# Layer 1's mixer: half of v and half of u as seven block products on normalized tiles

## The chip, the core and the metric

The kernel runs on one core of a Trainium2 chip. Its engines work side by side, each through its own list in order: TensorE (PE) multiplies, VectorE (DVE) and ScalarE (ACT) do elementwise work, GpSimd (POOL) some elementwise work and the issue of accumulating transfers, SyncE (SP) the issue of loads. They wait for each other by semaphores. The metric is the device time of one execution in microseconds (us).

## The reference

A trunk of two layers over 512 tokens of width 1024, in float32. Layer 0's mixer is a gated convolution beside a pooling, layer 1's a gMLP with spatial gating; each layer ends in a gated convolutional FFN of width 2816. What matters here is layer 1's mixer:

```python
def rms_norm(x, g):
    y = x * lax.rsqrt(jnp.mean(x * x, axis=-1, keepdims=True) + EPS)
    return y * g

def chunked_spatial_gating(u, v, sgu_norm, w_spatial, b_spatial):
    vn = rms_norm(v, sgu_norm).reshape(b, n, CHUNK, C_HEADS, C_HEAD_DIM)
    ws = w_spatial * mask                       # lower triangle
    gate = jnp.einsum('hts,bnshc->bnthc', ws, vn) + b_spatial.T[None, None, :, :, None]
    return u * gate.reshape(b, s, C_WIDTH)

xn = rms_norm(h, norm_mix[1])
proj = gelu(xn @ w_in_odd)                      # 1024 -> 2048
u, v = proj[..., :1024], proj[..., 1024:]
h = h + chunked_spatial_gating(u, v, ...) @ w_out_odd
```

## The kernel before

**Tiles.** The residual h lies as eight tiles `h[k]` of 128 features by 512 tokens. Each float32 operand of a matmul is split into two parts of the matmul's own type: `hi` is a copy by ACT, `lo` the remainder by DVE (`parts`, L131; `summed`, L122, gets the remainder by ACT and an accumulating transfer that POOL issues). A product of two such operands is three matmuls (`mm3`, L138): hi x hi, hi x lo, lo x hi. `hg[k]` holds the parts of `h[k]` times the norm's gain.

**The norm.** While the layer before ends, `Norm.add` (L179) makes the parts of `hg[k]` on ACT and DVE as soon as h[k] is added (L288), squares h[k] on ACT (L191) and adds the squares on POOL (L192, `ssq`). The factor r = 1/rms per token exists in two forms: as columns (`rstd_cols`, L205: four small matmuls over `ssq` into a bank called `ssc`, then a root) and spread over all partitions (`rstd_spread`, L195: four transposes into a bank called `ssr`, then a copy).

**Layer 1's mixer** (`mixer1`) computes v and u with tokens as output rows. Each is done in two halves of 512 columns, in the order v0, v1, u0, u1 (`in_group`, then `group`, L143): for each of eight feature tiles k and four token blocks j, `mm3` with 128x128 of `hg[k]` and a 128x512 piece of the weights, summed in four banks. That is 4 x 8 x 3 = 96 matmuls of 128x512 for each half. `hg` is not normalized, so r enters at the end as the scale of the Gelu on ACT; r's columns are made when the first bank of v0 is done. The spatial weights are loaded first, masked on POOL and turned by eight transposes inside v0 (`turn_spatial`). After v1 the columns of v's own norm give `vn`; after u0 come the eight spatial products (`spatial`, 3 matmuls each) and the first gatings (`gated`), and inside u1 the first four results are turned (`turned`) for the output projection `oo`.

**Layer FFNs.** They already use a form with seven block products for most of their width (`Ffn.both`): `Ffn.multiply` runs 4 x 3 matmuls of 128x256 for a product, and `Ffn.normalize` (L573) prepares normalized tiles, their parts and four block sums.

**What sets the order.** Loads go through SP's queue into four buffers (`raw`); a load is issued when the buffer's last reader is done. Weight parts have six buffers each. The program is recorded in the order of the code, and a scheduler then orders the instructions of each engine by its own costs, save those marked `inorder`; `behind` adds a constraint of order. The built order is fixed: on the chip each engine takes its list from the front. There are seven banks for products and one for small matters.

## Time and profile before

| | |
|---|---|
| timed runs, median | 997.9 us (997.45 to 998.35, three runs) |
| the profiled execution | 996.07 us |
| its span, first to last instruction | 994.4 us |
| mean granted TensorE clock | 0.998 |
| busy: PE, DVE, ACT, POOL | 99%, 70%, 53%, 10% |
| v0's first matmul | at 493.5 us |
| u0's first matmul | at 538.9 us |
| the last gelu of u1 starts | at 590.0 us |

The page of the profile is of one execution. Rows of a timeline give the start and the length in us, the engine, the line of the kernel, the operation, output<-inputs, the shape and a count; in brackets stands how long the engine had been idle before and what released it. A PE row's length holds the pipeline's depth, so the pace of matmuls is read from start to start.

### The profile page before, as it was taken

To read this page: it belongs to the slowest core of one execution; us is meant where nothing else is said; L and a number is where in the kernel's file an instruction comes from. 1 tells how busy PE (TensorE), PEld (TensorE's weight loads), DVE (VectorE), ACT (ScalarE), POOL (GpSimd) and SP (SyncE) were. 2 spreads that over 40 slices of the span, in tenths; PEclk is the share of its full clock that TensorE was granted. 3 is DMA by queue.
4 is the path that set the end of the run, shared out by engine and by line. 5 is a ranking of instruction groups with operands and counts; after the bars stand their busy time and mean duration, and the time that the engine had idled before them with its cause. 6 is when DMAs were issued, how large, how long until landed. Compare 5 with 4: busy or idle time off the path is not lost.

```text
span 994.4 us, 14683 instructions
## 1 busy us (share of the span) xinstructions
PE 983.6 (99%) x5811; PEld 872.0 (88%) x5811; DVE 699.4 (70%) x1053; ACT 523.9 (53%) x779; POOL 102.3 (10%) x120
## 2 busy tenths in 40 slices
PE   9999999999999999999999999999999999999997
PEld 6788888898989989899888888888989899898995
DVE  6887458967785877858943645399668768688676
ACT  5523346744653746537655344675546366363664
POOL 2131031200000000000300001211000010000100
PEclk9999999999999999999999999999999999999999
DMA  7342235554554645446333223435445456354542
GB/s 246 130 149 84 85 93 130 117 149 117 135 144 108 177 115 134 139 105 186 130 127 106 66 88 101 103 91 132 141 102 140 141 116 181 98 141 144 120 114 85
DMA packets 81904, 124.53 MB, mean 125 GB/s; under 512 B 4292, under 2 KB 53676, under 8 KB 81836
## 3 DMA queue, kind: packets, MB, share of 16 engines
q1 hardware_dynamic: 73004, 97.91, 30.8%
q0 software_dynamic: 6912, 23.07, 13.0%
q10 hardware_dynamic: 1920, 2.63, 0.8%
q8 instruction: 45, 0.74, 0.3%
q14 instruction: 23, 0.19, 0.1%
HBM read 98.42 MB, written 2.10 MB: 101 GB/s over the span
## 4 chain that ended last, share of the span: by engine, by line
PE 95%; DVE 2%; DMA 1%; issue 1%; ACT 0%; POOL 0%; SPq 0%; POOLq 0%; ACTq 0%
PE dn L139 4%; PE d L140 4%; PE d L139 4%; PE dn L140 4%; PE dn L141 4%; PE d L141 4%; PE gu L139 3%; PE gu L141 3%; PE gu L140 3%; PE v L139 1%; PE v L141 1%; PE u L139 1%; PE u L141 1%; PE oo L139 1%; PE oo L140 1%; PE oo L141 1%
## 5 line engine op out<-in xcount | busy, mean ns | idle before, releaser
L139 PE MATMUL dn<-whi_dn,a_hi 128*128 128x512 f32 x176 | 68.6, 390 | 0.0
L140 PE MATMUL d<-a_lo,whi_d 128*128 128x512 f32 x176 | 68.6, 390 | 0.0
L140 PE MATMUL dn<-wlo_dn,a_hi 128*128 128x512 f32 x176 | 68.6, 390 | 0.0
L141 PE MATMUL d<-a_hi,wlo_d 128*128 128x512 f32 x176 | 68.5, 389 | 0.0
L141 PE MATMUL dn<-whi_dn,a_lo 128*128 128x512 f32 x176 | 67.2, 389 | 0.0
L139 PE MATMUL d<-a_hi,whi_d 128*128 128x512 f32 x176 | 66.9, 390 | 0.0
L513 DVE SCALAR_TENSOR_TENSOR c<-rows,prm,c 128x512 f32<-128x512 f32 x88 | 65.4, 767 | 0.0
L127 POOL DMA_DIRECT2D wlo_g<-raw_g x22 | 19.1, 868 | 376.8 <-ACT wlo_g L126 362.6
L934 DVE TENSOR_TENSOR y<-dn,y 128x512 f32<-128x512 f32 x48 | 32.4, 685 | 23.3 <-PE dn L141 22.9
L126 ACT ACTIVATE wlo_g<-raw_g 128x1024 fp32r<-128x1024 f32 x22 | 23.2, 1055 | 42.3 <-PE dn L140 42.3
L135 DVE TENSOR_TENSOR wlo_u<-raw_u,whi_u 128x1024 fp32r<-128x1024 f32 x16 | 19.5, 1222 | 34.1 <-ACT whi_u L134 34.0
L519 ACT ACTIVATE s<-c,prm 128x512 f32<-128x512 f32 x44 | 30.9, 717 | 20.5 <-DVE c L513 20.4
L640 DVE TENSOR_TENSOR wlo_s34u<-s34u,whi_s34u 128x1024 fp32r<-128x1024 f32 x18 | 22.1, 1225 | 26.1 <-ACT whi_s34u L639 26.1
L639 ACT ACTIVATE whi_s12u<-s12u 128x1024 fp32r<-128x1024 f32 x18 | 18.9, 1051 | 39.5 <-PE d L140 33.7
L141 PEld LDWEIGHTS dn<-whi_dn,a_lo 128*128 128x128 f32 x176 | 33.0, 188 | 7.5 <-DVE a_lo L245 0.2
L140 PEld LDWEIGHTS d<-a_lo,whi_d 128*128 128x128 f32 x176 | 33.1, 188 | 7.2 <-DVE a_lo L245 0.2
L139 PEld LDWEIGHTS dn<-whi_dn,a_hi 128*128 128x128 f32 x176 | 33.1, 188 | 7.1 <-ACT a_hi L243 0.2
L288 DVE TENSOR_TENSOR h<-d,h 128x512 f32<-128x512 f32 x48 | 32.6, 684 | 9.3 <-PE d L141 9.3
L139 PEld LDWEIGHTS d<-a_hi,whi_d 128*128 128x128 f32 x176 | 32.9, 188 | 7.0
L141 PEld LDWEIGHTS d<-a_hi,wlo_d 128*128 128x128 f32 x176 | 33.0, 188 | 6.7
L140 PEld LDWEIGHTS dn<-wlo_dn,a_hi 128*128 128x128 f32 x176 | 33.1, 188 | 6.5
L192 POOL TENSOR_TENSOR ssq_f<-ssq_f,sq_f 128x512 f32<-128x512 f32 x14 | 18.9, 1348 | 180.8 <-ACT sq_f L191 145.9
(1195 smaller groups left out, 3414.8 us busy)
## 6 DMA issues: line engine op xcount, KB each, us to landing
raw_g<-in_w_ffn_gate_dram SPq DMA_DIRECT2D x36, 512.0 KB
raw_u<-in_w_ffn_up_dram SPq DMA_DIRECT2D x36, 512.0 KB
wlo_g<-raw_g POOLq DMA_DIRECT2D x22, 512.0 KB, 4.9
raw_d<-in_w_ffn_down_dram SPq DMA_DIRECT2D x22, 512.0 KB
raw_dn<-in_w_ffn_down_dram SPq DMA_DIRECT2D x22, 512.0 KB
wlo_u<-raw_u POOLq DMA_DIRECT2D x18, 512.0 KB, 5.0
raw_oe<-in_w_out_even_dram SPq DMA_DIRECT2D x8, 512.0 KB
raw_g<-in_w_ffn_gate_dram SPq DMA_DIRECT2D x16, 256.0 KB
```

Of the source, the lines that this page charges most:

```text
L126: nc.scalar.activation(lo, raw, AF.Copy, scale=-1.0)
L127: nc.gpsimd.dma_start(lo, raw, accum_op=ALU.add)
L135: behind(nc.vector.tensor_tensor(lo, raw, hi.bitcast(F32), ALU.subtract), after[0])
L139: nc.tensor.matmul(ps, lhs[0], rhs[0], start=start, stop=False)
L140: nc.tensor.matmul(ps, lhs[0], rhs[1], start=False, stop=False)
L141: nc.tensor.matmul(ps, lhs[1], rhs[0], start=False, stop=stop)
L192: nc.gpsimd.tensor_tensor(self.ssq, self.ssq, sq, ALU.add)
L288: nc.vector.tensor_tensor(h[k], ps, h[k], ALU.add)
L513: nc.vector.scalar_tensor_tensor(c, t[:, i : S + i], prm("cf", i * NF + ft), c, op0=ALU.mult, op1=ALU.add)
L519: nc.scalar.activation(s, c, AF.Silu, bias=self.prm("bf", ft))
L640: nc.vector.tensor_tensor(lo, src, hi.bitcast(F32), ALU.subtract)
L934: nc.vector.tensor_tensor(dst, ps, dst, ALU.add)
```

## The change

The first half of v (v0) stays a plain group, its feature tiles taken in the order 0, 4, 1, 5, 2, 6, 3, 7. r's columns are now made after 18 of its matmuls, and r is spread after 33. While v0 runs, `normalize(kp)` writes each pair of tiles again, normalized, in place in `hg[kp]` and `hg[kp + 4]`, and four sums and differences of their token halves (256 tokens each), with their parts, into `sums`; the first two pairs take `lo` by ACT and an accumulating transfer.

The second half of v (v1) and the first half of u (u0) are each computed by seven block products over blocks of 256 tokens, 512 features and 256 columns (`InProducts`), each of them in two halves of 128 tokens: 14 products of 4 x 3 matmuls of 128x256, with tokens as the stationary operand. The weights' sums are built in place in the raw buffers on DVE (L866 to L872 of the changed kernel). Seven weight parts take the place of four. Products 1, 6, 7 and 4 of a token half share a bank, which ACT copies out in between; DVE adds the others. Gelu comes without r's scale.

The second half of u (u1) stays a plain group on normalized tiles. The load of the spatial weights, their mask and their transposes move behind u0; all spatial products, the gatings of the first half and its transposes now stand between matmuls of u1 (`along`). `Ffn.multiply` becomes a wrapper of a free function `multiply` with the same instructions.

```diff
+    BANK = {1: "a", 6: "a", 7: "a", 4: "a", 5: "e", 3: "e", 2: "b"}
+    def multiply(banks, name, product, left, right):
+        at = BANK[product]
+        first = at not in banks
+        if first:
+            banks[at] = mm_bank(f"{name}{at}")
+        ps = banks[at][:, :HALF]
+        for kp in range(NP):
+            (a_hi, a_lo), (b_hi, b_lo) = left(kp), right(kp)
+            for l, r, end in ((a_hi, b_hi, False), (a_hi, b_lo, False),
+                              (a_lo, b_hi, kp == NP - 1)):
+                nc.tensor.matmul(ps, l, r, start=first, stop=end, skip_group_check=True)
+                first = False
+        return ps
...
+            chunks = {}
+            for kp in range(NP):
+                raw = wp.tile([P, 2, 512], F32, tag="raw", bufs=4, name=f"raw_v0_{kp}")
+                nc.sync.dma_start(raw, w[:, 1024:1536].rearrange(
+                    "(h k p) c -> p h k c", h=2, p=P)[:, :, kp])
+                hi, lo = parts(raw, 2, 512, f"v0_{kp}")
+                chunks[kp], chunks[kp + NP] = (hi[:, 0], lo[:, 0]), (hi[:, 1], lo[:, 1])
+            banks = {}
+            r = None
+            head = NK - 2
+            for i, j in ([(i, j) for i in range(head) for j in range(NT)]
+                         + [(i, j) for j in range(NT) for i in range(head, NK)]):
+                if (i, j) == (1, 2):
+                    norm.rstd_cols(inorder)
+                elif (i, j) == (2, 2):
+                    r = norm.rstd_spread(inorder)
+                k, cs = PAIRS[i], slice(j * P, (j + 1) * P)
+                if j not in banks:
+                    banks[j] = mm_bank(f"v0_{j}")
+                mm3(banks[j], (hg[k][0][:, cs], hg[k][1][:, cs]), chunks[k], i == 0, i == NK - 1)
+            work2 = [mp.tile([P, 2, S], F32, tag="v", bufs=4, name=f"nx{i}") for i in range(4)]
+            both = mp.tile([P, 4, S], F32, tag="u", bufs=2, name="nx4")
+            work2 += [both[:, :2], both[:, 2:]] * 2
...
+            sums = [[mp.tile([P, 2, 4, HALF], F32R, name=f"s{q}_{n}", **where)
+                     for n, where in enumerate(at)]
+                    for q, at in enumerate(((dict(tag="vn", bufs=4),) * 2,
+                                            (dict(tag="u", bufs=2), dict(tag="ws", bufs=1))))]
+            def halves(dst, src):
+                nc.scalar.activation(dst[0], src, AF.Copy)
+                nc.vector.tensor_tensor(dst[1], src, dst[0].bitcast(F32), ALU.subtract)
+            def normalize(kp):
+                x, t = work2[2 * kp], work2[2 * kp + 1]
+                for i, k in enumerate((kp, kp + NP)):
+                    nc.vector.scalar_tensor_tensor(x[:, i, :], h[k], prm1("mix", k), r,
+                                                   op0=ALU.mult, op1=ALU.mult)
+                halves(hg[kp], x[:, 0, :])
+                halves(hg[kp + NP], x[:, 1, :])
+                t = t.rearrange("p a (b c) -> p (a b) c", b=2)
+                a11, a21 = x[:, 0, :HALF], x[:, 0, HALF:]
+                a12, a22 = x[:, 1, :HALF], x[:, 1, HALF:]
+                nc.vector.tensor_tensor(t[:, 0, :], a21, a22, ALU.add)
+                nc.vector.tensor_tensor(t[:, 1, :], t[:, 0, :], a11, ALU.subtract)
+                nc.vector.tensor_tensor(t[:, 2, :], a11, a21, ALU.subtract)
+                nc.vector.tensor_tensor(t[:, 3, :], a12, t[:, 1, :], ALU.subtract)
+                hi, lo = (x[:, kp % 2] for x in sums[kp // 2])
+                if kp >= 2:
+                    halves((hi, lo), t)
+                    return
+                nc.scalar.activation(lo, t, AF.Copy, scale=-1.0)
+                nc.gpsimd.dma_start(lo, t, accum_op=ALU.add)
+                nc.scalar.activation(hi, t, AF.Copy)
+            SUM = {5: 0, 6: 1, 7: 2, 3: 3}
+            def tokens(product, i):
+                def at(kp):
+                    if product in SUM:
+                        cs = slice(i * P, (i + 1) * P)
+                        return tuple(x[:, kp % 2, SUM[product], cs] for x in sums[kp // 2])
+                    k = kp if product == 1 else kp + NP
+                    cs = slice((i + 2 * (product == 4)) * P, (i + 2 * (product == 4) + 1) * P)
+                    return hg[k][0][:, cs], hg[k][1][:, cs]
+                return at
+            class InProducts:
+                def __init__(self, name, c0, first=None):
+                    self.name, self.stat, self.first = name, {}, first
+                    self.raw = {}
+                    for i, j in ((0, 0), (1, 0), (0, 1), (1, 1)):
+                        self.raw[i, j] = fetch(
+                            w[i * 512 : (i + 1) * 512, c0 + j * HALF : c0 + (j + 1) * HALF]
+                            .rearrange("(k p) c -> p k c", p=P), 4, HALF, f"{name}_{i}{j}")
+                def plain(self):
+                    self.put(1, parts, (0, 0))
+                    self.put(2, summed, (1, 0))
+                def put(self, product, how, at):
+                    raw, a, b, name = self.raw[at]
+                    self.stat[product] = how(raw, a, b, f"{name}_{product}")
+                def rest(self):
+                    b11, b21, b12, b22 = (self.raw[at][0] for at in
+                                          ((0, 0), (1, 0), (0, 1), (1, 1)))
+                    behind(nc.vector.tensor_tensor(b12, b12, b11, ALU.subtract), self.first)
+                    self.put(5, parts, (0, 1))
+                    nc.vector.tensor_tensor(b12, b22, b12, ALU.subtract)
+                    self.put(6, parts, (0, 1))
+                    nc.vector.tensor_tensor(b11, b12, b11, ALU.subtract)
+                    self.put(7, parts, (0, 0))
+                    nc.vector.tensor_tensor(b21, b21, b12, ALU.subtract)
+                    self.put(4, parts, (1, 0))
+                    self.put(3, parts, (1, 1))
+                def run(self, out_, done):
+                    banks = ({}, {})
+                    e = {}
+                    for i, product in ((0, 1), (1, 1), (0, 2), (1, 2), (0, 6), (1, 6), (0, 5),
+                                       (0, 7), (1, 5), (1, 7), (0, 4), (0, 3), (1, 4), (1, 3)):
+                        hi, lo = self.stat[product]
+                        ps = multiply(banks[i], f"{self.name}_{i}", product, tokens(product, i),
+                                      lambda kp: (hi[:, kp, :], lo[:, kp, :]))
+                        c = {1: (0, 0), 2: (0, 0), 6: (0, 1), 3: (0, 1), 7: (1, 1), 5: (1, 1),
+                             4: (1, 0)}[product]
+                        dst = out_(i + 2 * c[0])[:, c[1] * HALF : (c[1] + 1) * HALF]
+                        if product in (1, 6):
+                            nc.scalar.copy(dst, ps)
+                        elif product == 5:
+                            e[i] = ps
+                        elif product == 7:
+                            nc.scalar.copy(dst, ps)
+                            self.last = nc.vector.tensor_tensor(dst, e[i], dst, ALU.add)
+                            nc.scalar.activation(dst, dst, AF.Gelu)
+                        elif product == 4:
+                            nc.scalar.activation(dst, ps, AF.Gelu)
+                            done(i + 2)
+                        else:
+                            nc.vector.tensor_tensor(dst, ps, dst, ALU.add)
+                        if product == 3:
+                            row = out_(i)
+                            nc.scalar.activation(row, row, AF.Gelu)
+                            done(i)
+            v1 = InProducts("v1", 1536)
+            v1.plain()
+            for kp in range(NP):
+                normalize(kp)
+            for t in range(NT):
+                nc.scalar.activation(v[t][:, :512], banks[t], AF.Gelu,
+                                     scale=norm.cols[:, t : t + 1])
+                v_square(0, t)
+            v1.rest()
...
+            v1.run(lambda t: v[t][:, 512:], lambda t: v_square(1, t))
+            u0 = InProducts("u0", 0, v1.last)
+            u0.plain()
...
             nc.vector.tensor_tensor(ssv[:, 0, :], ssv[:, 0, :], ssv[:, 1, :], ALU.add)
             rv = inv_sqrt_cols(ssv[:, 0, :], NT, "v")
...
+            v_normed(0)
...
-            in_group("u0", w, 0, False, u_done(0), 4)
-            for j in range(NK):
-                spatial(j)
-                if j < 4:
-                    gated(j)
-            def first_half(k):
-                if 2 <= k < 6:
-                    turned(k - 2)
-            in_group("u1", w, 512, False, u_done(1), 4, before=first_half)
+            u[0] = mp.tile([P, NT, S], F32, tag="u", bufs=2, name="u0")
+            u0.rest()
+            u0.run(lambda t: u[0][:, t, :], lambda t: None)
+            v_normed(1)
+            ws = wp.tile([P, NK, P], F32, tag="raw", bufs=4, name="ws")
+            nc.scalar.dma_start(ws, w_spatial[0].rearrange("h t s -> t h s"))
+            nc.gpsimd.affine_select(out=ws, in_=ws, pattern=[[0, NK], [-1, P]],
+                                    compare_op=ALU.is_ge, fill=0.0, base=0, channel_multiplier=1)
+            wsT = mp.tile([P, 2, NK, P], F32R, tag="ws", bufs=1, name="wsT")
+            wsT_hi, wsT_lo = wsT[:, 0], wsT[:, 1]
+            def turn_spatial(q):
+                ps = aux_bank(f"wst{q}")
+                for i in range(4):
+                    inorder(nc.tensor.transpose(ps[:, i * P : (i + 1) * P], ws[:, 4 * q + i, :],
+                                                ident))
+                hi = wsT_hi[:, 4 * q : 4 * q + 4, :]
+                pv = ps.rearrange("p (h t) -> p h t", t=P)
+                nc.scalar.activation(hi, pv, AF.Copy)
+                nc.vector.tensor_tensor(wsT_lo[:, 4 * q : 4 * q + 4, :], pv, hi.bitcast(F32),
+                                        ALU.subtract)
+            def along(k):
+                if k in (1, 2):
+                    turn_spatial(k - 1)
+                elif k == 4:
+                    for j in range(4):
+                        spatial(j)
+                        gated(j)
+                elif k in (6, 7):
+                    for j in (0, 1) if k == 6 else (2, 3):
+                        turned(j)
+                        spatial(j + 4)
+            def u1_done(t, ps):
+                nc.scalar.activation(u[1][:, t, :], ps, AF.Gelu)
+            u[1] = mp.tile([P, NT, S], F32, tag="u", bufs=2, name="u1")
+            in_group("u1", w, 512, False, u1_done, 4, before=along)
```

More of the change, by code (lines that the diff above doesn't have):

```diff
@@ L613, in moving @@
             return tuple(t[:, {4: 0, 5: 1}[product], :] for t in self.t41[kp])
-        BANK = {1: "a", 6: "a", 7: "a", 4: "a", 5: "e", 3: "e", 2: "b"}
         def multiply(self, banks, name, product, weights_):
-            at = self.BANK[product]
-            first = at not in banks
-            if first:
-                banks[at] = mm_bank(f"{name}{at}")
-            ps = banks[at][:, :HALF]
-            hi, lo = weights_
-            for kp in range(NP):
-                b_hi, b_lo = self.moving(product, kp)
-                a_hi, a_lo = hi[:, kp, :], lo[:, kp, :]
-                for l, r, end in ((a_hi, b_hi, False), (a_hi, b_lo, False),
-                                  (a_lo, b_hi, kp == NP - 1)):
-                    nc.tensor.matmul(ps, l, r, start=first, stop=end, skip_group_check=True)
-                    first = False
-            return ps
+            hi, lo = weights_
+            return multiply(banks, name, product, lambda kp: (hi[:, kp, :], lo[:, kp, :]),
+                            lambda kp: self.moving(product, kp))
         def unit(self, name):
@@ L761, in mixer1 @@
                                 .to_broadcast([P, 1, D]))
-            ws = mp.tile([P, NK, P], F32, tag="v", bufs=4, name="ws")
-            nc.scalar.dma_start(ws, w_spatial[0].rearrange("h t s -> t h s"))
-            nc.gpsimd.affine_select(out=ws, in_=ws, pattern=[[0, NK], [-1, P]],
-                                    compare_op=ALU.is_ge, fill=0.0, base=0, channel_multiplier=1)
-            wsT_hi = mp.tile([P, NK, P], F32R, name="wsT_hi")
-            wsT_lo = mp.tile([P, NK, P], F32R, name="wsT_lo")
@@ L768, in turn_spatial @@
-            def turn_spatial(k):
-                if k not in (3, 4):
-                    return
-                q = k - 3
-                ps = aux_bank(f"wst{q}")
-                for i in range(4):
-                    inorder(nc.tensor.transpose(ps[:, i * P : (i + 1) * P], ws[:, 4 * q + i, :],
-                                                ident))
-                hi = wsT_hi[:, 4 * q : 4 * q + 4, :]
-                pv = ps.rearrange("p (h t) -> p h t", t=P)
-                nc.scalar.activation(hi, pv, AF.Copy)
-                nc.vector.tensor_tensor(wsT_lo[:, 4 * q : 4 * q + 4, :], pv, hi.bitcast(F32),
-                                        ALU.subtract)
@@ L782, in mixer1 @@
-            rcol = []
-            def r_of(t):
-                if not rcol:
-                    rcol.append(norm.rstd_cols())
-                return rcol[0][:, t : t + 1]
+            chunks = {}
[5 more added lines that the diff above has]
+                chunks[kp], chunks[kp + NP] = (hi[:, 0], lo[:, 0]), (hi[:, 1], lo[:, 1])
@@ L789, in mixer1 @@
+            work2 = [mp.tile([P, 2, S], F32, tag="v", bufs=4, name=f"nx{i}") for i in range(4)]
+            both = mp.tile([P, 4, S], F32, tag="u", bufs=2, name="nx4")
+            work2 += [both[:, :2], both[:, 2:]] * 2
             v = [mp.tile([P, D], F32, tag="v", bufs=4, name=f"v{t}") for t in range(NT)]
             ssv = mp.tile([P, 4, PAD], F32, name="ssv")[:, :, :NT]
-            def v_done(half):
-                def done(t, ps):
-                    dst = v[t][:, half * 512 : (half + 1) * 512]
-                    nc.scalar.activation(dst, ps, AF.Gelu, scale=r_of(t))
-                    sq = tp.tile([P, S], F32, tag="sq", name=f"sqv{half}_{t}")
-                    nc.scalar.activation(sq, dst, AF.Square, accum_out=ssv[:, half, t : t + 1])
-                return done
@@ L800, in mixer1, with v_square @@
-            in_group("v0", w, 1024, False, v_done(0), 2, before=turn_spatial)
-            in_group("v1", w, 1536, False, v_done(1), 4)
+            def v_square(half, t):
+                sq = tp.tile([P, S], F32, tag="sq", name=f"sqv{half}_{t}")
+                nc.scalar.activation(sq, v[t][:, half * 512 : (half + 1) * 512], AF.Square,
+                                     accum_out=ssv[:, half, t : t + 1])
+            sums = [[mp.tile([P, 2, 4, HALF], F32R, name=f"s{q}_{n}", **where)
+                     for n, where in enumerate(at)]
+                    for q, at in enumerate(((dict(tag="vn", bufs=4),) * 2,
+                                            (dict(tag="u", bufs=2), dict(tag="ws", bufs=1))))]
@@ L805, in mixer1, with v_normed @@
             vn = []
-            for half in range(2):
+            def v_normed(half):
                 hi = mp.tile([P, NT, S], F32R, tag="vn", bufs=4, name=f"vnh{half}")
@@ L815, in mixer1 @@
                 vn.append((hi, lo))
+            v_normed(0)
             u, gt, mix = {}, {}, {}
-            def u_done(half):
-                u[half] = mp.tile([P, NT, S], F32, tag="u", bufs=2, name=f"u{half}")
-                def done(t, ps):
-                    nc.scalar.activation(u[half][:, t, :], ps, AF.Gelu, scale=r_of(t))
-                return done
             def by_chunk(ap):
```

## Prediction

> **What bounds the kernel now.** I read the page first: the busy shares and the chain that ended last.

> ```profile
> PE 983.6 (99%) x5811; PEld 872.0 (88%) x5811; DVE 699.4 (70%) x1053; ACT 523.9 (53%) x779; POOL 102.3 (10%) x120
> ...
> PE 95%; DVE 2%; DMA 1%; issue 1%; ACT 0%; POOL 0%; SPq 0%; POOLq 0%; ACTq 0%
> ```

> TensorE is busy for 99% of the span and carries 95% of the chain. Averages hide stages, so I read next the windows over layer 1's mixer (columns: window, length, then busy time and instruction count of PE, PEld, DVE, ACT, POOL, then the granted clock).

> ```profile
> 493.50:515.30 21.80, 21.80 (x105) 18.17 (x104) 12.55 (x16) 10.90 (x14) 4.62 (x4) 1.00 0.47 152
> 515.30:538.90 23.60, 23.60 (x105) 19.55 (x105) 3.71 (x4) 13.63 (x26) 0.00 (x0) 1.00 0.25 82
> 538.90:564.00 25.10, 25.10 (x112) 20.78 (x112) 14.45 (x23) 16.82 (x23) 0.00 (x0) 1.00 0.30 94
> 564.00:590.00 26.00, 26.00 (x124) 21.54 (x123) 11.64 (x17) 7.40 (x11) 0.00 (x0) 1.00 0.22 72
> ```

> In both halves of v and u PE is busy for the whole window, at full clock. Nothing there is waiting that the change could take away; it can gain only by shortening PE's own list, and it loses each wait it brings in. VectorE (DVE) has 3.7 of 23.6 us busy in the second half of v, which is the cover the change spends.

> **What PE saves.** The timeline of PE gives the pace of a 128x512 matmul, the chain that of a 128x256 one.

> ```profile
> 493.49 0.39 PE L139 MATMUL v<-whi_v,hgh 128*128 128x512 f32 x1
> ...
> 497.57 0.39 PE L139 MATMUL v<-whi_v,hgh 128*128 128x512 f32 x1
> ```
> ```profile
> 203.31 1.44 PE u_4a L630 x12
> ```

> From 493.49 to 497.57 stand 18 matmuls: 4.08 / 18 = 0.227 us. Twelve half-width ones take 1.44 us: 0.120 us each, more than half of 0.227. A changed group turns 4 outputs x 8 tiles x 3 = 96 full matmuls (21.76 us) into 14 products x 4 pairs x 3 = 168 half ones (20.16 us): 1.60 us, and 3.20 us for v's second and u's first half. An eighth fewer multiplications is thus worth only 7%. I take 0.120 although the operands change sides (tokens stationary, weights moving), because the shape is the same.

> New on PE are four transposes that spread the row factor r. Layer 0's FFN has the same step:

> ```profile
> 152.94 0.60 PE L199 MATMUL ssr_f<-ident,rc_f0c 128*128 128x128 f32 x4
> 153.30 0.48 PE L139 MATMUL gu<-hgh,whi_g 128*128 128x512 f32 x1
> 153.61 0.40 PE L140 MATMUL gu<-hgl,whi_g 128*128 128x512 f32 x1
> ```

> From 152.94 to 153.61 less one matmul is 0.44 us. The spatial matmuls and other transposes only move. PE's list alone: -3.20 + 0.44 = -2.76 us.

> **New wait 1: the sum of squares.** In the kernel before, r's column form was formed late; now PE stops for it after 18 matmuls of v's first half, at 497.57 by the row above. It needs the last add of squares on POOL, behind h7's add on DVE:

> ```profile
> 484.21 2.89 DVE L182 SCALAR_TENSOR_TENSOR hgl<-h,prm,hgh 128x512 fp32r<-128x512 f32 x2
> 487.03 0.68 DVE L288 TENSOR_TENSOR h<-d,h 128x512 f32<-128x512 f32 x1
> 487.63 1.71 DVE L135 TENSOR_TENSOR wlo_v<-raw_v,whi_v 128x1024 fp32r<-128x1024 f32 x1
> 489.26 1.78 DVE L182 SCALAR_TENSOR_TENSOR hgl<-h,prm,hgh 128x512 fp32r<-128x512 f32 x1
> 490.96 0.68 DVE L288 TENSOR_TENSOR h<-d,h 128x512 f32<-128x512 f32 x1
> 492.43 0.75 DVE L182 SCALAR_TENSOR_TENSOR hgl<-h,prm,hgh 128x512 fp32r<-128x512 f32 x1 [0.79 <-ACT hgh L181]
> 493.10 0.68 DVE L288 TENSOR_TENSOR h<-d,h 128x512 f32<-128x512 f32 x1
> 494.58 0.75 DVE L182 SCALAR_TENSOR_TENSOR hgl<-h,prm,hgh 128x512 fp32r<-128x512 f32 x1 [0.79 <-ACT hgh L181]
> 495.25 0.68 DVE L288 TENSOR_TENSOR h<-d,h 128x512 f32<-128x512 f32 x1
> ```
> ```profile
> 489.13 1.36 POOL L192 TENSOR_TENSOR ssq_m<-ssq_m,sq_m 128x512 f32<-128x512 f32 x1 [0.87 <-ACT sq_m L191]
> ...
> 497.36 1.38 POOL L192 TENSOR_TENSOR ssq_m<-ssq_m,sq_m 128x512 f32<-128x512 f32 x1 [0.85 <-ACT sq_m L191]
> ```

> The sum is complete at 498.74, 3.49 after h7's add starts. So PE would wait 1.17 us even if nothing moved. But in the built order two steps have come in ahead of h7: the first difference of v1's raw weights (128x1024, between hgl2 and hgl3) and the low part of v1's first weights (between h6 and hgl6). Steps of that size follow each other in 1.14 us:

> ```profile
> 176.90 2.34 DVE L135 TENSOR_TENSOR wlo_d<-raw_d,whi_d 128x1024 fp32r<-128x1024 f32 x2
> ```

> The second falls partly into the 0.79 us of waiting before hgl6 and costs 0.35; the first costs 1.14, for behind it h4 to h7 queue on a DVE whose rows follow each other without a pause from 484.21 to 490.96. To that comes the collision with POOL: hgl takes 1.78 us at 489.26 and 0.75 at 492.43, and the long one starts inside POOL's add at 489.13. [...] The rows show some meeting and some not.

> By the rows one collision costs up to 1.03. So h7 is 1.5 to 2.5 us later; I take 1.85, a collision one time in three. Wait 1 = 1.17 + 1.85 = 3.0 us; bounds 0 (every collision gone) and 4.7 (one more collision). It has no cover: PE's queue is in order, and r and all that follows hang behind.

> **New wait 2: the token sums.** After the transposes PE has 63 matmuls of v's first half (14.28 us), then products 1 and 2 (48 x 0.120 = 5.76) and 22 matmuls of product 5 before it needs the last token sum: 22.68 us. In that time DVE must normalize all four pairs. Its durations stand in layer 0's FFN:

> ```profile
> 153.58 0.59 ACT L202 COPY rstd_f<-ssr_f 128x512 f32<-128x512 f32 x1 [2.23 <-PE ssr_f L199]
> ```
> ```profile
> 154.20 1.41 DVE L578 SCALAR_TENSOR_TENSOR x<-h,prm,rstd_f 128x512 f32<-128x512 f32 x2 [2.05 <-ACT rstd_f L202]
> ...
> 155.87 1.28 DVE L583 TENSOR_TENSOR hgl<-x,hgh 128x512 fp32r<-128x512 f32 x2
> ...
> 159.21 0.42 DVE L591 TENSOR_TENSOR t<-t,x 128x256 f32<-128x256 f32 x1
> 159.54 0.74 DVE L578 SCALAR_TENSOR_TENSOR x<-h,prm,rstd_f 128x512 f32<-128x512 f32 x1
> ```

> Start to start: 0.66 for a scaling, 0.60 for a low part, 0.33 for a quarter sum. The built order has, up to the last low part of the sums, 8 x 0.66 + 8 x 0.60 + 16 x 0.33 + 6 x 1.14 (two sums' low parts, three raw weight sums, one weight's low part) = 22.2 us, some 0.4 for the last copy on ScalarE (ACT), and 0.8 for r's own copy: 23.4 + 0.2 of landing. Against 22.68 that is a wait of about 1.0 us; 0.3 to 2 if either list is 3% off.

> **New wait 3: a bank.** Product 6 goes into the bank of product 1, which ACT must have copied out. In ACT's order that copy stands behind the last sum's copy and three weight copies:

> ```profile
> 469.25 1.05 ACT L134 ACTIVATE whi_d<-raw_d 128x1024 fp32r<-128x1024 f32 x1
> 470.20 1.04 ACT L134 ACTIVATE whi_v<-raw_v 128x1024 fp32r<-128x1024 f32 x1
> ...
> 203.60 0.35 ACT L690 COPY rows<-g_4a 128x256 f32<-128x256 f32 x1
> ```

> From the end of that sum's copy: ACT needs 3 x 0.95 + 0.35 = 3.2 less 0.1 of overlap; PE needs the low part on DVE (1.22) and two matmuls, 1.46. Wait 3 = 1.65 us; both sides hang on the same event, so 1.3 to 1.9.

> **At no cost, and with what cover.** u0's raw weights load when v1's sums release the buffers; v1's 14 products (20 us) cover 512 KB loads and their parts, else one low part each, 1.2 us. The spatial weights, their load on ACT's queue and POOL's selection move behind u0; u0's products cover them. Spatial products and transposes between u1's matmuls wait for single copies: 0.3 us in all, up to 1. POOL's accumulating transfers are issued pairs ahead of use.

> **Sum.** -3.20 + 0.44 + 3.0 + 1.0 + 1.65 + 0.3 = +3.2 us. On the profiled execution (996.07 us, span 994.4 and 1.67 around it) 999.3; that one lies 1.8 under the median 997.9 of the three timed runs, so for the median I say 1001.1 us.

> **Rivals.** (a) The other side: h7 comes in time. If DVE meets no POOL add, its list loses stalls like that at 489.26, up to 1.0 us each, and h7's add starts as soon as PE has finished its bank, at about 493.7 (its last d matmul starts one step before 493.49 and takes 0.39); then wait 1 is 0 and the sum +0.2: 998.1, not slower. It decides at 497.57 - 3.49 = 494.1. Against it: the same queue met POOL in this trace and got longer. 20%. (b) Waits 2 and 3 as well are covered: -2.8, 995.1. That needs 2.6 us less on DVE and ACT than their rows add up to: 7%. (c) ACT becomes the second bound through both product stages: product 7 of the second token half waits for the copy of product 6 behind two weight copies (1.9 us against 1.44 of cover); 0.65 us at four places, 2.6: 1003.7. For it: ACT has 16.8 of 25.1 us busy already and gets more. 12%. (d) The clock. The first matmuls of the kernel, after idleness, run slowly:

> ```profile
> L56 PE MATMUL clock<-idle 128*128 128x512 bf16 x8 | 3.6, 631 | 1.3 <-DVE idle L53 1.3
> ```

> Eight took 3.6 us; warm ones would need 8 x 0.227 = 1.8. If the long idleness of wait 1 brings this slow start again, the loss is 1.8 us, partly given back in wait 2: 1002.9. Against it: PEclk stands at 1.00 in every window above; but PE never paused there. 5%. [...]

> **How the numbers follow.** The forecast has 56%, its own range +1.7 to +5 us. A measurement can tell about 0.2%, 2.0 us. Faster is (b), 7%; the same is (a) and the forecast's low edge, 22%; slower the rest, 71%. The range leaves out (b) and the extremes of (c): 998.0 to 1004.6.

> **What would show it.** Right: in PE's waits a wait of ssc for POOL near 3 us, some 2.6 us before products 5 and 6 of v1, none in u0; half matmuls at 0.120. Wrong: ssc under 1.2 us, h7 not later than 1.75 us after v's first matmul, product 6 starting unhindered, or the granted clock under 1.00 after the first wait.

## The result, and the profile after

| | before | after |
|---|---|---|
| timed runs, median (six of each) | 998.12 us (997.45 to 1001.01) | 1005.25 us (1003.75 to 1006.6) |
| ratio, 95% interval | | 1.0067 (1.0051 to 1.0083) |
| the profiled execution, its span | 996.07, 994.4 us | 1006.13, 1004.4 us |
| mean granted clock | 0.998 | 0.993 |
| from v0's first matmul to the output projection's (oo) first | 96.30 us | 105.08 us |

The change is slower by 0.67%. The direction was forecast, the size was not: 1005.25 lies 0.65 above the range's end of 1004.6. The profiled executions differ by 10.06 us. Of that 1.21 is there before layer 1's mixer begins (v0 starts at 494.70 instead of 493.49), 8.78 is the mixer, and what follows is unchanged: from oo's first matmul to the end of the span both need 404.6 us. So what the profile shows of the loss is to be found in the 105 us of the mixer. The medians differ by 7.13 us, less than these two mixers: the six runs of after spread from 1003.75 to 1006.6, and only the one of 1006.13 has a profile.

The page of after: PE has more busy time than before (988.2 against 983.6 us), though its list was meant to shrink by 2.76, and the row of the granted clock has a place where it isn't 9.

```profile
PE 988.2 (98%) x5959; PEld 881.8 (88%) x5959; DVE 734.3 (73%) x1111; ACT 545.3 (54%) x818; POOL 106.3 (11%) x124
...
PEclk9999999999999999999989999999999999999999
```

PE's waits in after (total, times, longest): the three forecast waits are there, with a fourth at the turning of the spatial weights. The 4.0 of the first row is two waits, the 3.4 is layer 1's.

```profile
PE ssc_m L209 <- POOL ssq_m L192: 4.0, 2, 3.4
PE v_0a L499 <- ACT v L888: 1.3, 1, 1.3
...
PE wst L987 <- DVE wsT L992: 0.6, 1, 0.6
PE v_0e L499 <- DVE s L807: 0.5, 1, 0.5
```

They are too small for 8.78. The windows over the mixer, cut at the same events as before, show the rest (length; busy time and count of PE, PEld, DVE, ACT, POOL; the granted clock; DMA):

```profile
494.70:515.30 20.60, 17.17 (x70) 13.99 (x69) 12.08 (x21) 10.21 (x15) 4.76 (x4) 0.83 0.24 61
515.30:538.90 23.60, 21.74 (x130) 19.74 (x129) 23.21 (x36) 21.03 (x34) 1.72 (x2) 0.93 0.42 105
538.90:564.00 25.10, 25.10 (x211) 25.10 (x210) 16.94 (x27) 20.91 (x39) 1.17 (x2) 1.00 0.45 134
564.00:599.78 35.78, 35.16 (x184) 29.38 (x184) 24.54 (x33) 18.15 (x27) 0.79 (x1) 1.00 0.40 132
```

In the first two windows the clock is 0.83 and 0.93, where every window before had 1.00. Finer windows, cut every 3.41 us, show where:

```profile
494.64:498.06 3.42, 3.42 (x16) 2.83 (x16) 3.30 (x4) 2.32 (x4) 2.25 (x2) 1.00 0.59 184
498.06:501.47 3.41, 0.89 (x4) 0.38 (x3) 2.33 (x3) 1.80 (x3) 0.84 (x2) 1.00 0.09 34
501.47:504.88 3.41, 2.51 (x10) 2.41 (x11) 0.33 (x2) 2.83 (x4) 1.66 (x2) 0.50 0.40 77
504.88:508.30 3.42, 3.42 (x9) 2.65 (x9) 0.66 (x5) 1.06 (x1) 0.00 (x0) 0.50 0.41 77
508.30:511.71 3.41, 3.41 (x18) 2.79 (x18) 1.93 (x3) 0.67 (x2) 0.00 (x0) 1.00 0.00 0
...
532.20:535.61 3.41, 1.55 (x11) 1.14 (x10) 3.38 (x3) 3.37 (x5) 0.00 (x0) 1.00 0.46 154
535.61:539.02 3.41, 3.41 (x18) 3.41 (x18) 3.05 (x5) 1.96 (x3) 0.00 (x0) 0.50 0.85 268
539.02:542.44 3.42, 3.42 (x30) 3.42 (x30) 0.42 (x1) 2.25 (x5) 0.86 (x1) 1.00 0.95 270
```

The clock is exactly half for 6.8 us after wait 1 and for 3.4 us after waits 2 and 3. Both stretches start a whole number of 3.41 us steps apart (34.1 us, ten steps). PE counts as busy there, so no view of waits shows it; the instruction counts do: 9 and 18 in windows that hold 18 and 30 at full clock. PE's timeline shows the price of a matmul:

```profile
498.56 0.39 PE L141 MATMUL v<-whi_v,hgl 128*128 128x512 f32 x1
502.37 1.87 PE L209 MATMUL ssc_m<-small,ssq_m 128*128 128x1 f32 x8 [3.43 <-POOL ssq_m L192]
...
505.10 0.63 PE L141 MATMUL v<-whi_v,hgl 128*128 128x512 f32 x1
505.53 0.63 PE L139 MATMUL v<-whi_v,hgh 128*128 128x512 f32 x1
...
532.71 0.28 PE L499 MATMUL v_1e<-wlo_v,s 128*128 128x256 f32 x1
533.51 0.39 PE L499 MATMUL v_0e<-whi_v,s 128*128 128x256 f32 x1 [0.52 <-DVE s L807]
533.73 0.28 PE L499 MATMUL v_1e<-whi_v,s 128*128 128x256 f32 x1
535.35 0.39 PE L499 MATMUL v_0a<-whi_v,s 128*128 128x256 f32 x1 [1.33 <-ACT v L888]
```

Start to start a 128x512 matmul takes 0.43 us (505.10 to 505.53) instead of 0.227. The waits, start to start less the pace: wait 1 is 502.37 - 498.56 - 0.227 = 3.59 us (the row's 3.43 counts from the end of the last matmul); wait 2 is 0.68, wait 3 1.49 (pace 0.120). The four matmuls of the sum over the squares stand in the trace as eight one-column rows: 1.73 us here from the first to the next matmul (502.37 to 504.10), 0.81 in the kernel before.

Why h7 was late is in DVE's and POOL's rows of after:

```profile
486.69 2.16 DVE L866 TENSOR_TENSOR raw_v<-raw_v,raw_v 128x1024 f32<-128x1024 f32 x1
...
495.80 1.54 DVE L135 TENSOR_TENSOR wlo_v<-raw_v,whi_v 128x1024 fp32r<-128x1024 f32 x1
497.26 1.77 DVE L182 SCALAR_TENSOR_TENSOR hgl<-h,prm,hgh 128x512 fp32r<-128x512 f32 x1
498.96 0.68 DVE L288 TENSOR_TENSOR h<-d,h 128x512 f32<-128x512 f32 x1
```
```profile
484.52 5.47 POOL L192 TENSOR_TENSOR ssq_m<-ssq_m,sq_m 128x512 f32<-128x512 f32 x3 [25.06 <-ACT sq_m L191]
...
494.96 1.30 POOL L192 TENSOR_TENSOR ssq_m<-ssq_m,sq_m 128x512 f32<-128x512 f32 x1 [0.87 <-ACT sq_m L191]
497.11 1.39 POOL L192 TENSOR_TENSOR ssq_m<-ssq_m,sq_m 128x512 f32<-128x512 f32 x1 [0.85 <-ACT sq_m L191]
501.06 1.26 POOL L192 TENSOR_TENSOR ssq_m<-ssq_m,sq_m 128x512 f32<-128x512 f32 x1 [2.57 <-ACT sq_m L191]
```

h7's add starts 498.96 - 494.70 = 4.26 us after v0 begins, against 1.76 before: 2.50 later (forecast 1.85). The two added steps took 2.16 and 1.54 where the prediction had 1.14, and hgl6 (497.26) took 1.77 where it took 0.75 before: by POOL's rows each of the three ran beside an add there. The last add, at 501.06, ends at 502.32, and PE goes on at 502.37.

### The profile page after: what moved, and what is told of

It is laid out like the page before. It is cut to its first block, busy times and chain, and to the rows that moved or that the text cites. A ratio compares the mean times of both kernels' runs of the same rounds, so it can differ in the third digit from the quotient of the medians.

```text
span 1004.4 us, 15096 instructions
## 1 busy us (share of the span) xinstructions
PE 988.2 (98%) x5959; PEld 881.8 (88%) x5959; DVE 734.3 (73%) x1111; ACT 545.3 (54%) x818; POOL 106.3 (11%) x124
## 4 chain that ended last, share of the span: by engine, by line
PE 92%; DVE 3%; ACT 2%; DMA 1%; issue 1%; POOL 0%; SPq 0%; ACTq 0%; POOLq 0%; DVEq 0%
PE dn L139 4%; PE dn L141 4%; PE dn L140 4%; PE d L139 4%; PE d L140 4%; PE d L141 4%; PE gu L139 3%; PE gu L140 3%; PE gu L141 3%; PE oo L141 1%; PE oo L139 1%; PE oo L140 1%; PE oe L140 1%; PE oe L139 1%; PE oe L141 1%; PE g_12a L499 1%
## 5 line engine op out<-in xcount | busy, mean ns | idle before, releaser
L140 PE MATMUL d<-a_lo,whi_d 128*128 128x512 f32 x176 | 68.7, 390 | 0.0
L139 PE MATMUL dn<-whi_dn,a_hi 128*128 128x512 f32 x176 | 68.7, 390 | 0.0
L140 PE MATMUL dn<-wlo_dn,a_hi 128*128 128x512 f32 x176 | 68.6, 390 | 0.0
L139 PE MATMUL d<-a_hi,whi_d 128*128 128x512 f32 x176 | 66.9, 390 | 0.0
L140 PEld LDWEIGHTS d<-a_lo,whi_d 128*128 128x128 f32 x176 | 33.1, 188 | 7.3 <-DVE a_lo L245 0.2
L288 DVE TENSOR_TENSOR h<-d,h 128x512 f32<-128x512 f32 x48 | 32.6, 683 | 9.4 <-PE d L141 9.3
L139 PEld LDWEIGHTS dn<-whi_dn,a_hi 128*128 128x128 f32 x176 | 33.1, 188 | 7.1 <-ACT a_hi L243 0.2
L139 PEld LDWEIGHTS d<-a_hi,whi_d 128*128 128x128 f32 x176 | 32.9, 188 | 7.0
L140 PEld LDWEIGHTS dn<-wlo_dn,a_hi 128*128 128x128 f32 x176 | 33.1, 188 | 6.6
L135 DVE TENSOR_TENSOR wlo_dn<-raw_dn,whi_dn 128x1024 fp32r<-128x1024 f32 x22 | 26.8, 1220 | 12.9 <-ACT whi_dn L134 12.9
L135 DVE TENSOR_TENSOR wlo_d<-raw_d,whi_d 128x1024 fp32r<-128x1024 f32 x22 | 26.8, 1219 | 11.3 <-ACT whi_d L134 11.3
```

Source lines behind the costliest of these rows:

```text
L135: behind(nc.vector.tensor_tensor(lo, raw, hi.bitcast(F32), ALU.subtract), after[0])
L139: nc.tensor.matmul(ps, lhs[0], rhs[0], start=start, stop=False)
L140: nc.tensor.matmul(ps, lhs[0], rhs[1], start=False, stop=False)
L288: nc.vector.tensor_tensor(h[k], ps, h[k], ALU.add)
```

## The experiments

Theories, as the expectations name them. **A**: the lost time is the three waits and, behind them, matmuls at half clock. **B**: the two DVE steps that came in ahead of h7 are not what makes wait 1. **C**: the slow matmuls come from what runs beside them (DVE, ACT, transfers), or from the new schedule, not from the idleness.

**e1_early: the two DVE steps behind the last low part.**

```diff
-            v1 = InProducts("v1", 1536)
-            v1.plain()
+            v1 = InProducts("v1", 1536, norm.last)
+            v1.plain((norm.last, None))
...
```

`norm.last` is the step that makes hgl7; the lines left out hand it on.

> The first difference of v1's raw weights and the low part of v1's first weights are ordered on DVE behind the last low part of hg, so that h7's add no longer queues behind them; all else as in the changed kernel. Theory A (waits, and a clock that halves after them): wait 1 falls from 3.6 us to 1.2 to 1.8, the granted clock stays at 1.00 through the rest of v's first half, wait 2 grows by up to 2 us because PE comes sooner to the token sums, wait 3 and the second slow stretch stay: 1000.5 to 1002.5 us against 1005.2. Theory B (the added DVE steps are not what makes the sum of squares late): wait 1 stays above 3 us and the time at 1005. Theory C (the slow matmuls come from what runs beside them, not from the pause): wait 1 falls but the matmuls after it still take 0.43 us: 1003.5.

Measured 1000.6 us, 1.0031 (1.0019 to 1.0043) of the kernel before. Wait 1 fell from 3.59 to 1.10 us, so the two steps made 2.5 of it and B is out. Wait 2 did not grow as expected but fell to 0.3; wait 3 stayed. The profiled execution (997.58 us) had no half clock in the mixer, against the expectation of a second stretch:

```profile
PE ssc_m L209 <- POOL ssq_m L192: 1.5, 2, 0.9
```
```profile
497.76:501.17 3.41, 2.60 (x15) 2.32 (x16) 3.31 (x5) 2.74 (x5) 1.63 (x2) 1.00 0.18 35
```

The other eleven ran from 997.16 to 1003.26, and the longer their time, the lower their mean clock (0.998 to 0.999 up to 998.4; 0.997 at 999.4; 0.995 and 0.996 from 1000.5 to 1002.2; 0.993 at 1003.3). By these clocks the same program with the same list had the half clock in some executions and not in others.

**e2_copy: the bank's copy ahead of three weight copies.** The weight parts of products 7, 4 and 3 are recorded after product 1's copy and their ACT copies put behind it (`more`, left out below, does this).

```diff
                         if product in (1, 6):
-                            nc.scalar.copy(dst, ps)
+                            copied = nc.scalar.copy(dst, ps)
+                            if (i, product) == (1, 1) and self.name == "v1":
+                                self.more(copied)
...
```

> On ACT the copies of v1's last three weight parts (products 7, 4, 3) are ordered behind the copies of product 1's two banks; all else as in the changed kernel. Theory A: wait 3 (1.5 us) falls under 0.2; the pause before product 6 shrinks from 2.2 us in all to 0.7 and the second slow stretch (3.4 us at half clock, about 1.7 us lost) goes: 1002 us. If wait 2 alone brings the slow stretch: 1003.7. If the slow matmuls of product 6 come from their operands and not from the pause: 1003.7 too, with 0.21 us from start to start in product 6 right after unbroken work. Rival (the bank is waited for whatever ACT's order): 1005.

Measured 1001.76 us, 1.004 (1.0027 to 1.0052). Windows of 3.41 us around wait 1, in its profile:

```profile
499.00:502.42 3.42, 0.11 (x1) 0.00 (x0) 1.56 (x3) 2.58 (x4) 1.20 (x1) 1.00 0.01 2
502.42:505.83 3.41, 3.29 (x12) 3.00 (x13) 0.83 (x5) 2.04 (x3) 0.88 (x2) 0.50 0.62 119
505.83:509.24 3.41, 3.41 (x10) 2.64 (x9) 0.94 (x1) 1.06 (x1) 0.00 (x0) 0.50 0.19 35
509.24:512.66 3.42, 3.42 (x19) 2.82 (x18) 1.59 (x3) 1.11 (x2) 0.00 (x0) 1.00 0.00 0
```

Wait 1 and its 6.8 us at half clock are as in after; waits 2 and 3 and the second stretch are gone, and so is the wait at the spatial weights. That wait 2 went too was not expected (0.7 was to stay), and it isn't the copy's doing alone: in the list as built, product 6's 24 matmuls now stand ahead of the last four of product 5, and before the last two of these PE had waited. The mixer took 100.80 us, 4.28 less than after. That the halves can be taken away one by one speaks for A.

**e3_fill: matmuls in place of the pause.** Sixteen 128x512 matmuls into a bank that nobody reads, ahead of the sum over the squares. Nothing else is edited, but the built order moved a little: the sum stands after 19 of v0's matmuls instead of 18, r's transposes after 31 instead of 33.

```diff
                 if (i, j) == (1, 2):
+                    filler = aux_bank("filler")
+                    for _ in range(16):
+                        inorder(nc.tensor.matmul(filler, hg[0][0][:, :P], hg[0][0], start=True,
+                                                 stop=True))
                     norm.rstd_cols(inorder)
```

> Sixteen matmuls of 128x512 whose result nobody reads are put before the four that form r's columns, so that PE works (16 x 0.227 = 3.6 us) while it would wait; nothing else changes, and the sum of squares comes no sooner. Theory A: PE is free of the pause, the clock stays at 1.00 there, the 3.1 us that the slow matmuls cost go; of these 0.8 (r's columns) shorten everything behind, the rest is partly given back in wait 2, which grows from 0.7 to 2 or 3 us: 1002.5 to 1004.5. Theory C (not the pause but what runs beside makes the matmuls slow): 16 us after v's first matmul they still take 0.43 us, and the time is 1005 or more.

Measured 1000.33 us, 1.0028 (1.0017 to 1.0038). The mixer takes 100.17 us, 4.91 less than after's, with more work in PE's list. The filler takes the 3.6 us of wait 1, the clock stays 1.00. From the start of the sum over the squares to the 31st matmul of v0 behind it the kernel after needs 11.10 us, this one 8.26: the first stretch at half clock costs 2.84. The steps on DVE, ACT and POOL run beside the matmuls here as there, so they do not make them slow.

```profile
500.40:503.81 3.41, 3.41 (x20) 2.75 (x19) 0.83 (x5) 2.67 (x5) 1.38 (x2) 1.00 0.50 96
```

The time lies under the expected 1002.5 to 1004.5, because two more things went its way. Wait 2 was to grow and is down to 0.1 us: from r's transposes to the matmul behind that wait it is 23.94 us here and 23.93 in after, but PE has two more of v0's matmuls to do in between. And the clock stayed at 1.00 after wait 3, which is still 1.49 us long. So not all of the 4.91 us is the filler's.

**e4_pause: a pause in the kernel before.** r's columns made ahead of v0's first matmul.

```diff
+    gate = [None]
...
-        nc.tensor.matmul(ps, lhs[0], rhs[0], start=start, stop=False)
+        behind(nc.tensor.matmul(ps, lhs[0], rhs[0], start=start, stop=False), gate[0])
...
+                if k == 0:
+                    rcol.append(norm.rstd_cols(put_gate))
```

> The kernel before, with one thing moved: r's columns are formed ahead of v's first matmul instead of behind its first half, so that PE has one pause of about 5.2 us (the sum of squares ends at 498.74, the first matmul would start at 493.49) and no other; no block products. Theory A: 5.2 us of pause plus a stretch of 3.4 to 6.8 us at half clock, 1.7 to 3.4 us more: 1005 to 1006.8 against 998.1. If a pause costs only itself: 1003.3.

Measured 1005.08 us, 1.0081 (1.0068 to 1.0093). Nothing of the change is in it but a pause:

```profile
492.82 0.39 PE L143 MATMUL d<-a_hi,wlo_d 128*128 128x512 f32 x1
498.29 1.01 PE L211 MATMUL ssc_m<-small,ssq_m 128*128 128x1 f32 x4 [5.08 <-POOL ssq_m L194]
```
```profile
494.09:497.50 3.41, 0.00 (x0) 0.00 (x0) 3.25 (x4) 3.39 (x6) 1.86 (x2) 1.00 0.64 206
497.50:500.91 3.41, 2.62 (x10) 2.52 (x11) 1.69 (x4) 1.08 (x3) 1.83 (x2) 0.50 0.80 253
500.91:504.33 3.42, 3.42 (x9) 2.65 (x9) 1.65 (x4) 0.64 (x1) 0.00 (x0) 0.50 0.12 33
```

(The second row stops at the view's end; the sum has eight such matmuls.) The pause is 492.82 to 498.29 less 0.227, 5.24 us. From the last d matmul to oo's first the run needs 104.70 us (492.82 to 597.52), the kernel before 96.52 (493.27 to 589.79): 8.18 more, so that 2.9 us come on top of the pause. That is near the 2.84 of e3_fill; the 6.8 us at half clock would lose 3.4 if PE had work in all of them, and 0.8 of them still belong to the pause. None of the new schedule is needed for it: C is out.

**e5_both and e6_late.** The first has the edits of e1 and e2. The second has also the following, so that PE reaches the sum over the squares when it is done (`rooted["m1c"]` is the last small step of r on DVE):

```diff
-                if (i, j) == (1, 2):
+                if (i, j) == (2, 0):
                     norm.rstd_cols(inorder)
...
-            v1 = InProducts("v1", 1536, norm.last)
+            v1 = InProducts("v1", 1536, rooted["m1c"])
...
-                    self.put(5, parts, (0, 1))
+                    self.put(5, summed if self.name == 'v1' else parts, (0, 1))
```

> The edits of e1_early and e2_copy together: the two added DVE steps behind h7's low part, and the three weight copies behind the copy of product 1's bank. Theory A (the added time is the waits, and the halved clock after them): wait 1 is 1.1 us as in e1_early, wait 2 0.3, wait 3 at most 0.2, no slow stretch in any run because no idle time of 2 us is left; the mixer takes 96.30 - 2.76 + 1.1 + 0.3 + 0.2 + 0.5 (rest) = 95.6 us, the median 996.7, and the runs no longer spread by their clock (e1_early 997.2 to 1003.3). Theory C (the new schedule itself brings the slow stretch, whatever the waits): a slow stretch stays in part of the runs and the median stays at or above 999.

> e5_both with wait 1 taken away as well: the sum over the squares stands six matmuls later in PE's list (after 24 of v's first half), the first difference of v1's raw weights follows the last small step of r on DVE, and product 5's weights get their low part by ACT and an accumulating transfer. Theory A: wait 1 falls from 1.1 to 0 to 0.3; r is ready at the same time or 0.5 to 1 us earlier; wait 2 gets some of it back (DVE's list behind r is as long as before): 0.5 to 1.0 together with wait 3. Mixer 94.8 to 95.4 us, the median 996.0 to 996.6, under the kernel before's 997.4. Rival: whatever wait 1 loses comes back in full at the token sums, since DVE's chain sets the end; then 996.7 as e5_both.

e5_both: 997.59 us, 0.9993 (0.9984 to 1.0003), no difference from the kernel before that these runs can tell. The waits fell as expected (1.10 us at wait 1, no other forecast wait above 0.25). But the mixer took 96.91 us instead of 95.6: the half clock came back in its profile, after a pause of only 1.1 us, which in e1_early's profile had left the clock at 1.00:

```profile
496.55:499.96 3.41, 2.47 (x16) 1.89 (x15) 2.99 (x3) 3.39 (x5) 1.79 (x3) 1.00 0.06 24
499.96:503.37 3.41, 3.41 (x9) 2.63 (x9) 1.86 (x6) 1.63 (x3) 0.50 (x1) 0.50 0.76 145
503.37:506.79 3.42, 3.42 (x19) 2.81 (x18) 2.10 (x3) 0.94 (x3) 0.00 (x0) 1.00 0.05 8
```

Its twelve runs lie between 995.43 (clock 0.999) and 999.25 (0.995), against the expectation that they would no longer spread. Theory A held for the waits; that it takes a pause of 2 us was wrong.

e6_late: 995.07 us, 0.9969 (0.9960 to 0.9978): a little faster than the kernel before, and 0.9 us under what was expected. Its windows over the mixer, cut at v0, v1, u0, u1 and oo:

```profile
495.25:518.41 23.16, 23.16 (x109) 19.31 (x108) 19.40 (x37) 17.98 (x24) 6.91 (x7) 1.00 0.49 102
518.41:539.41 21.00, 20.71 (x169) 20.28 (x168) 18.18 (x25) 19.82 (x38) 0.86 (x1) 1.00 0.54 139
...
sum 94.74, PE 94.43 PEld 84.62 DVE 75.88 ACT 70.33 POOL 8.86; mean PE 23.61 PEld 21.15 DVE 18.97 ACT 17.58 POOL 2.21
```

v1 in products takes 21.0 us with its last 0.4 us of wait 2 in it. The mixer is 1.56 us shorter than before, at full clock. The sum over the squares no longer waits, it starts 0.23 us behind the matmul ahead of it:

```profile
500.46 0.39 PE L141 MATMUL v<-whi_v,hgl 128*128 128x512 f32 x1
500.69 0.95 PE L209 MATMUL ssc_m<-small,ssq_m 128*128 128x1 f32 x8
```

What wait 1 lost came back in part: PE stands still for 0.23 us inside product 1 (520.10) and for 0.38 at the token sums (526.54), where e5_both's v1 had no gap above 0.1, so some 0.6 of 1.1. The rival, that all of it comes back, is out. Of the 2.76 us that PE's list was to gain, 1.56 are measured; these two waits are 0.6 of the difference, the rest lies in gaps of 0.2 us and less.

**e7_part_fill: a single unbroken pause of 2 us.** e2_copy with seven unread matmuls.

```diff
+                    for _ in range(7):
+                        inorder(nc.tensor.matmul(filler, hg[0][0][:, :P], hg[0][0], start=True,
+                                                 stop=True))
```

> e2_copy with seven unread 128x512 matmuls ahead of the sum over the squares in place of e3_fill's sixteen: they take 1.6 us, so that wait 1 is one unbroken pause of about 2.0 us with nothing after it. If the clock is halved by any idle time of about 2 us, broken or not: the slow stretch stays, the time is that of e2_copy, 1001.8. If an unbroken 2.0 us is below the limit (and the second stretch of the changed kernel came from something else): no slow stretch, 1001.8 - 3.1 = 998.7. Runs of both kinds would put the limit at about 2 us.

Measured 1000.07 us, 1.0017 (1.0006 to 1.0028), runs from 997.57 to 1001.7, between the two cases of the expectation (1001.8 and 998.7). The pause was 1.79 us; its profiled execution (1000.11) had one window at half clock behind it, not two:

```profile
499.97:503.38 3.41, 1.78 (x12) 1.56 (x12) 0.73 (x2) 3.39 (x4) 2.08 (x2) 1.00 0.10 19
503.38:506.79 3.41, 3.41 (x9) 2.66 (x9) 1.83 (x5) 1.35 (x3) 0.00 (x0) 0.50 0.71 135
```

**Second profiles: e10_early_again, e9_late_again, e8_before_again.** The same three programs once more.

> e1_early once more: its first profile had no slow stretch and 997.6 us, the median of its runs was 1000.6. If the clock is set window by window (3.41 us each, a window with too few columns makes the next one slow), this execution shows the same pauses (1.1; 0.3 and 1.5 us) at another phase of the windows, and in three cases of four a slow stretch of 3.4 us behind one or both of them, at 999.4 to 1003; the window ahead of each slow one holds under about 3200 columns, all others more. If the slow stretch came from the length of a pause alone, the same pauses would give the same clock as before, 997.6.

999.28 us, the mixer 97.59 us, and again no half clock in it; the expected stretch did not come. The same pauses lay in these windows, and by chance at the same phase of the 3.41 us grid as in the first profile: the pauses come 1.95 to 1.97 us later than there, the windows 1.96. So this execution could not tell a limit on the length of a pause from one that depends on the phase; e5_both's profile, with the same pause at another phase, does.

```profile
499.72:503.13 3.41, 2.59 (x15) 2.32 (x16) 3.32 (x5) 2.76 (x5) 1.65 (x2) 1.00 0.17 34
...
527.02:530.44 3.42, 1.97 (x15) 1.56 (x13) 3.27 (x4) 3.42 (x6) 0.00 (x0) 1.00 0.48 153
530.44:533.85 3.41, 3.36 (x28) 3.36 (x29) 3.37 (x5) 2.04 (x4) 0.00 (x0) 1.00 0.87 280
```

The expectation's other half, the limit on columns, held; the table below has it. The runs of e1_early with the longest times have no profile, so their half clock is read from their mean clock alone.

> e6_late once more, for a second profile: mixer 94.7 us again, no slow stretch between 10 us and the last 10 us whatever the phase of the clock's windows, since no window there streams fewer than 3900 columns; the time 994.6 to 996.3 by where the first stage begins.

994.35 us, the mixer 94.69 us, no half clock: e6_late's shape stands.

> The kernel before once more, for a second profile. Where do executions of it differ by up to 3 us? If in the clock: a slow stretch of 3.4 us somewhere (the eight spatial transposes at 561 us stream few columns) in an execution of 998 us or more. If at the start (loads, the first transposes): the distances from layer 1's mixer to the end are as in the first profile, 96.3 and 404.6 us, and only the first marks move.

997.47 us, the mixer 96.31 us, full clock through the spatial transposes. It began v0 1.35 us later than the first profile, and was already 1.6 us later at 34 us: these two executions differ at the start, not in the mixer. So of e6_late's 0.31% (3.1 us) the profiles show 1.56 to 1.6 us in the mixer, and the rest isn't found in them.

**What sets the half clock.** In every trace the stretches begin and end on a grid of 3.41 us, at a phase that differs from execution to execution; in after the clock changes at 501.47, 508.30, 535.61 and 539.02, that is two, eight and one step apart (6.83, 27.31 and 3.41 us). I counted for each window of the grid the columns that went through PE (512 or 256 for a matmul from its row's start, cut matmuls in part). A full window holds 7,700 (3.41 us at 512 columns in 0.227).

| kernel, window with its pause | columns | clock in the next window |
|---|---|---|
| e2_copy, 499.00 (whole window idle) | 0 | 0.50 |
| e7_part_fill, 499.97 | 1,450 | 0.50 |
| after, 498.06 | 1,640 | 0.50 |
| after, 532.20 (waits 2 and 3) | 2,190 | 0.50 |
| e5_both, 496.55 | 3,160 | 0.50 |
| e10_early_again, 527.02 | 3,235 | 1.00 |
| e3_fill, 527.70 (wait 3) | 3,235 | 1.00 |
| e1_early, 525.06 | 3,310 | 1.00 |
| e1_early, 497.76 (pause cut in two by the grid) | 3,560 | 1.00 |

The limit fits each case above. Wait 1 in after empties most of one window (1,640 columns are left) and, with the eight one-column matmuls behind it, of the next (about 1,000): two half windows. In e5_both the 1.1 us pause and the 0.9 us of those one-column matmuls fell into one window (3,160), in e1_early's profile the grid cut off the pause's first 0.3 us (3,560), and in e3_fill the window with wait 3 held just enough (3,235). e6_late has no window of the mixer near the limit (none under 3,900).

## Why the prediction was right or wrong

| step | forecast | measured |
|---|---|---|
| PE's own list | -2.76 | -2.76 taken, pace 0.120 in u0 as forecast |
| wait 1 | 3.0 (0 to 4.7) | 3.59 |
| wait 2 | 1.0 (0.3 to 2) | 0.68 |
| wait 3 | 1.65 (1.3 to 1.9) | 1.49 |
| spatial waits | 0.3 (to 1) | 0.95 (0.76 before the spatial transposes, 0.2 behind the first results' transposes) |
| half clock after wait 1 | 0 (1.8 in rival d, 5%) | 2.84 |
| half clock after waits 2 and 3 | not named | 1.65 |
| sum | +3.2 | +8.4, of 8.78 |

(The second stretch: 18 half-width matmuls at 0.214 instead of 0.120 us, 1.7; 1.65 with the first and last in part.)

**Right:** that PE's list gains only 2.8 us because a half-width matmul costs more than half (0.120 us against 0.227); that three waits take its place, in their order and with their releasers; that h7 behind two added DVE steps and their meetings with POOL makes wait 1 (e1_early: 2.5 of 3.59), though three steps met an add (2.16, 1.54 and 1.77 us long, against 1.14, 1.14 and 0.75) where one meeting in three was counted (h7 is 2.50 later, not 1.85); that wait 3 is ACT's copy behind three weight copies (e2_copy takes it away). The sum of the three waits was 5.65 forecast and 5.76 measured; that it is so near is partly luck, since wait 1 was 0.59 longer and the other two together 0.48 shorter.

**Wrong: the step that gave the clock 5% and, in the likeliest case, nothing.** Two things failed in it. The condition: it asked for a "long idleness", and no row of the kernel before showed how long, since PE never paused in the windows read. The runs show no such length: 1.10 us had half clock behind it (e5_both), wait 3 of 1.49 had not (e3_fill). They show a grid window of 3.41 us, with half clock behind up to 3,160 columns and full clock behind 3,235 and more; by that count a pause of 3.0 us, with the 0.9 us of one-column matmuls behind it, leaves too few in one window at nearly every phase of the grid, and waits 2 and 3 together lost 2.2 us inside 2.5 (2,190 columns left). With that limit half clock was to be expected after wait 1, and possible after waits 2 and 3. The price: 1.8 us was read from eight matmuls at the kernel's start; wait 1 reaches across two windows, so it was 2.84, and a second stretch added 1.65. The two stretches are 4.5 of the 5.6 us between +3.2 and +8.78; wait 1's size is 0.6 more and the spatial waits 0.65, with 0.5 back from waits 2 and 3; 0.3 stays without a row.

**Rivals:** (a) and (b) did not happen, h7's add starts at 498.96 where (a) needed 494.1. (c) did not: no wait for ACT's copies at product 7 shows among PE's waits, and the windows of u0 have PE busy throughout. The sign "the granted clock under 1.00 after the first wait" was named as what would make the prediction wrong, and did.

## What to carry to other kernels

In these runs a wait of PE has two prices, its length and the half clock behind it. Work out for each pause how many columns its 3.41 us window still holds (here half clock came behind up to 3,160, full clock behind 3,235 and more), counting one-column matmuls as idle, and add up pauses that stand close together. Here a pause of 1 to 2 us (e1_early, e5_both, e7_part_fill) had the half clock behind it or not by its phase, so a profile without the half clock doesn't clear it, and a second profile can fall on the same phase: look at the spread of times and at the mean clock of all runs. Here block products paid only once the elementwise work that they need was ready: ordering a few small things (two DVE steps, three ACT copies, the place of the sum over the squares in PE's queue) and moving one low part from DVE to ACT and a transfer turned 0.67% slower into 0.31% faster.

## What was not expected of the hardware

Half clock does not need an idle window: 1.1 us of pause with 0.9 us of one-column matmuls, 3,160 columns of 7,700, was enough (e5_both). Unread matmuls in the place of a pause can be worth more than nothing: e3_fill's mixer did 3.6 us of useless work and was 4.9 us shorter than after's, 2.84 of it by the clock behind wait 1. And one program ran from 997.2 to 1003.3 us; in the two of its executions that have a profile (e1_early) the waits are the same to 0.01 us (wait 1 1.105 and 1.107, wait 3 1.498 and 1.493).
